# An encoder block on one core: the z of branch A by seven products, three pairs in phases, product sums kept in PSUM

## The chip, the core and the metric

One NeuronCore of a Trainium2 chip runs the whole program. The metric is the time of one execution in microseconds of the device; several runs are made and the median is told. Five engines work beside each other: TensorE (PE in the profile) multiplies matrices into PSUM, VectorE (DVE) and GpSimd (POOL) do elementwise work, ScalarE (ACT) activations and copies, SyncE (SP) issues loads. PSUM has banks of 128 partitions by 512 float32; a product tile here is one of them.

## The reference, cut

One block over 1024 tokens and 16 learned meta tokens, width 1024, float32:

```python
h = concat(meta, x)                      # 1040 x 1024
proj = rmsnorm(h, pre_norm_g) @ w_in + b_in
qa, ka, va, za, qb, kb, vb, zb, ga, gb = split(proj)
oa = diff_attention(qa, ka, va, ...)     # branch A: 4 heads, dense, its result normalised
ob = windowed_gqa(qb, kb, vb, ...)       # branch B: 8 heads, keys within 128
ya = (oa * silu(za)) @ w_out_a
yb = (ob * silu(zb)) @ w_out_b
mixed = sigmoid(ga) * ya + sigmoid(gb) * yb
out = (h + rmsnorm(mixed @ w_out, post_norm_g))[16:]
```

`za` and `zb` have 512 columns, `ga` and `gb` 1024. Meta tokens are needed as keys and values only, not in z, the gates or the output.

## The kernel before

Each float32 matrix product is made of three passes with operands split into a high and a low part (`hi`, `lo`): hi by hi, hi by lo, lo by hi, summed in PSUM. A split is a copy on ACT (`hi`) and a subtraction on another engine (`lo`); the helper `split` (L790) takes that engine as an argument, POOL if none is named. `hn` is the normalised input, transposed, in two parts; `hn[p][1]` holds the second half of the tokens.

The stages in order: norms and projections; branch B, whose gate z is projected as filler; branch A, head by head, with the next head's projections or z of branch B as filler between the steps of the softmax; then, from L720 on, what this change is about:

- **z of branch A** (L900 to L910): four slabs of 128 columns by `proj` (L143), each two chunks of 512 tokens, each chunk 24 matmuls of 128x512 at L151: 192 in all. The first slab takes the PSUM room `mm` of the attention stage, so the scheduler of the framework may put it between the attention's last steps. `gate_a` (L876) makes silu and multiplies with `oa`, which is loaded from `oa_d`.
- **Input sums**, `combos` (L793): the gates are made by a recursion with seven products in place of eight, which wants four sums of blocks of the input, `f1` to `f4` in tiles t1 (f1), t2 (f2), t4 (f4) and t3 (f3). Each is made in two halves of 128x1024 by two or three DVE operations, and split, its lo half on POOL. One piece is taken at each chunk of z.
- **The gates GA and GB** (L913): four pairs of 128-column slabs each, by `seven` (L829). A pair loads four quarters of its weights (two tiles `wr4` of 512 KB), makes sums of them on DVE (`ws`, L837), splits each of seven operands (`wh` on ACT, `wl` on POOL) and runs seven products P1 to P7 of twelve matmuls (L862) into seven PSUM tiles. The products are added up by DVE into SBUF tiles (L871) in the order that the lists SEVEN, FIRST and LAST give, seven sums and one ACT copy (L869) a pair. Before the first P6 the rest of `combos` is run.
- **Mix** (L966) multiplies the gated branches with `w_out_a` and `w_out_b`, and the **output stage** (`out_pair`, L1027) runs four pairs of seven products, then the sum of squares (ACT, L1049), the product with the norm's weights (L1051) and the final product and residual (L1070). The very last product P4 is made in two halves of 256 columns, each in a PSUM tile of its own, and is added on DVE to a tile in SBUF before L1049 reads it.

Engines take their instructions in the program's order; the framework's scheduler sets that order from the order of the code and priorities, and a tile that is written again waits for its readers. In branch B's first block the 16 meta keys are a block of their own: `VBM` and the transposed scores give two products (hi and lo) at L445.

## Time and profile before

| | |
|---|---|
| median of 3 runs | 908.79 us (908.16 to 908.87) |
| profiled execution, time | 907.95 us |
| its span | 906.1 us |
| PE busy | 858.2 us, 95% |
| DVE, ACT, POOL busy | 680.0, 488.8, 380.4 us |
| matmuls | 4670 |

The span is what the hardware profiler sees of one execution; the execution's own time holds a little more around it. PE's clock of 0.990 is its granted mean as a share of full speed (2.4 GHz).

### The profile page before, as it was taken

To read this page: it belongs to the slowest core of one execution; us is meant where nothing else is said; L and a number is where in the kernel's file an instruction comes from. 1 tells how busy PE (TensorE), PEld (TensorE's weight loads), DVE (VectorE), ACT (ScalarE), POOL (GpSimd) and SP (SyncE) were. 2 spreads that over 40 slices of the span, in tenths; PEclk is the share of its full clock that TensorE was granted. 3 is DMA by queue.
4 is the path that set the end of the run, shared out by engine and by line. 5 is a ranking of instruction groups with operands and counts; after the bars stand their busy time and mean duration, and the time that the engine had idled before them with its cause. 6 is when DMAs were issued, how large, how long until landed. Compare 5 with 4: busy or idle time off the path is not lost.

```text
span 906.1 us, 13766 instructions
## 1 busy us (share of the span) xinstructions
PE 858.2 (95%) x4670; PEld 733.9 (81%) x4670; DVE 680.0 (75%) x1432; ACT 488.8 (54%) x975; POOL 380.4 (42%) x482
## 2 busy tenths in 40 slices
PE   4799999999999999999999999399999999999995
PEld 2797988888888898899888887288888888887784
DVE  6735668767988988997877699975444476959897
ACT  4635567766868768877766532344444540114432
POOL 6224543545021212221222189555454555826553
PEclk9999999999999999999999999699999999999998
DMA  8321110215122121021111153464511366311223
GB/s 262 105 50 45 56 57 19 89 43 133 36 71 68 47 72 68 25 71 48 47 65 48 47 185 117 163 210 161 178 56 47 131 231 207 94 63 47 94 95 138
DMA packets 64318, 85.85 MB, mean 95 GB/s; under 512 B 5248, under 2 KB 49294, under 8 KB 64248
## 3 DMA queue, kind: packets, MB, share of 16 engines
q1 hardware_dynamic: 56640, 60.28, 21.1%
q10 hardware_dynamic: 7576, 24.67, 7.9%
q8 instruction: 37, 0.61, 0.3%
q14 instruction: 33, 0.27, 0.1%
q0 software_dynamic: 32, 0.02, 0.0%
HBM read 60.63 MB, written 19.00 MB: 88 GB/s over the span
## 4 chain that ended last, share of the span: by engine, by line
PE 63%; DVE 21%; ACT 7%; issue 5%; POOL 1%; DMA 1%; SPq 0%; DVEq 0%; ACTq 0%; POOLq 0%
PE mm L151 21%; PE pp L862 17%; PE pp L966 9%; PE pv L627 3%; DVE sb L588 3%; PE pv L445 2%; PE pT L432 2%; PE pT L615 2%; PE s L585 2%; DVE sb L598 2%; ACT sb L591 2%; PE s L586 2%; ACT sb L597 1%; DVE ws L837 1%; DVE TB L885 1%
## 5 line engine op out<-in xcount | busy, mean ns | idle before, releaser
L151 PE MATMUL mm<-hn,wh 128*128 128x512 f32 (+2 forms) x896 | 203.6, 356 | 2.9 <-ACT vT L347 1.9
L139 POOL TENSOR_SCALAR wh<-wr 128x256 fp32r<-128x256 f32 x124 | 63.5, 528 | 265.9 <-PE mm L151 237.4
L151 PEld LDWEIGHTS mm<-hn,wh 128*128 128x128 f32 x896 | 145.1, 192 | 19.2 <-ACT vT L347 2.1
L140 POOL TENSOR_TENSOR wl<-wr,wh 128x256 fp32r<-128x256 f32 x124 | 107.4, 890 | 19.4 <-PE mm L151 17.4
L151 PE MATMUL mm<-hn,wl 128*128 128x512 f32 (+2 forms) x448 | 101.5, 353 | 0.0
L792 POOL TENSOR_TENSOR wl<-ws,wh 128x512 fp32r<-128x512 f32 x48 | 71.6, 1501 | 66.0 <-ACT wh L791 52.2
L591 ACT ACTIVATE sb<-sb,st 128x1040 f32<-128x1040 f32 x64 | 74.3, 1162 | 35.2 <-DVE st L588 34.4
L862 PE MATMUL pp<-t,wh 128*128 128x512 f32 (+1 forms) x296 | 73.2, 390 | 15.6 <-ACT wh L791 15.6
L862 PE MATMUL pp<-hn,wh 128*128 128x512 f32 x320 | 79.8, 391 | 0.0
L151 PEld LDWEIGHTS mm<-hn,wl 128*128 128x128 f32 x448 | 73.7, 191 | 7.6
L862 PEld LDWEIGHTS pp<-t,wh 128*128 128x128 f32 x296 | 55.5, 191 | 28.2 <-ACT wh L791 16.9
L588 DVE CUSTOM_DVE_ANT_0 sb<-s,U,st 128x346 f32<-128x346 f32 x128 | 73.1, 574 | 5.8
L871 DVE TENSOR_TENSOR c<-c,pp 128x512 f32<-128x512 f32 x70 | 47.4, 682 | 38.5 <-PE pp L862 36.7
L862 PEld LDWEIGHTS pp<-hn,wh 128*128 128x128 f32 x320 | 60.1, 188 | 13.2
L585 PE MATMUL s<-K,Q 128*128 128x346 f32 (+1 forms) x192 | 65.8, 345 | 0.9 <-DVE st L588 0.4
L586 PE MATMUL s<-K,Q 128*128 128x346 f32 (+1 forms) x192 | 61.3, 321 | 0.0
L598 DVE SCALAR_TENSOR_TENSOR sb<-sb,st 128x1040 f32<-128x1040 f32 x32 | 43.9, 1372 | 13.2 <-ACT sb L597 12.9
L413 ACT ACTIVATE sb<-sb,st 128x385 f32<-128x385 f32 (+2 forms) x64 | 37.5, 588 | 22.6 <-DVE st L410 20.3
L417 POOL TENSOR_SCALAR sb<-sb,st 128x384 f32<-128x384 f32 (+2 forms) x64 | 35.5, 568 | 32.5 <-DVE st L415 32.4
L791 ACT ACTIVATE wh<-ws 128x512 fp32r<-128x512 f32 x48 | 29.7, 625 | 35.0 <-PE pp L862 20.1
L410 DVE CUSTOM_DVE_ANT_0 sb<-s,TB,nsink 128x384 f32<-128x384 f32 (+2 forms) x64 | 35.4, 580 | 16.6 <-PE s L408 15.0
L617 DVE TENSOR_TENSOR al<-pT,ah 128x512 fp32r<-128x512 f32 x64 | 43.7, 686 | 3.6 <-ACT ah L616 2.9
(212 smaller groups left out, 1928.7 us busy)
## 6 DMA issues: line engine op xcount, KB each, us to landing
wr<-in_w_in_dram SPq DMA_DIRECT2D x96, 128.0 KB, 2.5
wr<-in_w_in_dram SPq DMA_DIRECT2D x16, 512.0 KB, 3.6
K<-K ACTq DMA_DIRECT2D x16, 260.0 KB, 3.5
xt<-in_x_dram SPq DMA_DIRECT2D x8, 512.0 KB, 7.1
sg_d<-TB ACTq DMA_DIRECT2D x8, 512.0 KB, 2.6
w<-in_w_out_dram SPq DMA_DIRECT2D x4, 1024.0 KB, 5.5
room<-sg_d SPq DMA_DIRECT2D x8, 512.0 KB, 4.8
fx<-in_x_dram SPq DMA_DIRECT2D x8, 512.0 KB, 4.6
```

Of the source, the lines that this page charges most:

```text
L139: pool.tensor_scalar(hi, raw, 1.0, 1.0, ALU.mult, ALU.mult)
L140: pool.tensor_tensor(lo, raw, hi, ALU.subtract)
L151: pe.matmul(ps[:, :n], lhsT=w[k // 4][:, k % 4, :], rhs=hslice(part, k, st, n), start=(i == 0), stop=(i == 3 * KC - 1))
L585: pe.matmul(s, lhsT=q, rhs=KH[:, m, o:o + n], start=True, stop=False)
L586: pe.matmul(s, lhsT=q, rhs=KL[:, m, o:o + n], start=False, stop=True)
L588: dve.tensor_tensor_reduce(out=sb[:, o:o + n], in0=s, in1=back(U, u0 + o, n), scale=-0.125, scalar=lim, op0=ALU.add, op1=ALU.min, accum_ou ...
L591: act.activation(sb, sb, AF.Exp, bias=st[:, m:m + 1], scale=-1.0, accum_out=st[:, 2 + m:3 + m])
L598: dve.scalar_tensor_tensor(sbs[0], sbs[0], st[:, 4:5], sbs[1], ALU.mult, ALU.add)
L792: lo_eng.tensor_tensor(t[1][:, k], x, t[0][:, k], sub)
L862: pe.matmul(x[n][:, cs], lhsT=w[:, k], rhs=b[n][part][:, k, cs], start=(i == 0), stop=(i == 11))
L871: dve.tensor_tensor(x[o][:, cs], *src, add)
L966: pe.matmul(py, lhsT=w[:, k, :], rhs=g[h][:, k], start=(i == 0), stop=(i == 11))
```

## The change

- z of branch A is made in two pairs of seven products in place of four slabs of two chunks: 168 matmuls in place of 192.
- The two pairs of z and the first pair of GA go in phases: `head` (P1, P2, P3, which use blocks of the input as they are) of all three, then `middle` (P6, P5) of all three, then `tail` (P7, P4). The weights are loaded again for each phase by `quarters`.
- Product sums run on in PSUM: a later product is added onto the bank of an earlier one, which ACT copies out first (`copy`) where its own value is needed. A pair has three DVE sums and three ACT copies in place of seven and one.
- `combos` has t1's and t2's lo halves on DVE, f3 ahead of f4, and is no longer tied to the z chunks.
- Output stage: the first pair in the same phases, the others in the new plain order; the last P4's halves lie in one PSUM tile, and the last result is read out of PSUM.
- Meta keys of branch B: hi and lo stand at partitions 0 and 64 of one operand of 80 rows, so one product does both; POOL zeroes the operands early.

The core of the diff, whose new class takes the place of `seven` and the three lists:

```diff
-    VBM = sbp.tile([MT, 2, P], F32R, tag="am", name="vbm", bufs=1)
+    VBM = sbp.tile([80, 2, P], F32R, tag="sh", name="vbm", bufs=1)
...
-        n, last = 0, 2 * len(blocks) - 1
+        n, last = 0, 2 * len(blocks) - (i > 0)
...
+        if i == 0:
+            pe.matmul(pv[:, :256], lhsT=VBM[:, g, :], rhs=am, start=False, stop=True)
...
-            split(t1, x, k)
+            split(t1, x, k, dve)
...
-            split(t2, x, k)
+            split(t2, x, k, dve)
...
-        for f in (f1, f2, f4, f3):
-            yield from halves(f)
+        halves(f1, True)
+        yield
+        halves(f2, False)
+        yield
+        ys = xs[:]
+        halves(f3, True)
 
         for j in range(2):
             split(t3, xs[j], slice(2 * j, 2 * j + 2))
         yield
+        xs[:] = ys
+        halves(f4, False)
+        yield
...
+        def mul(self, n, ps=None, cuts=(slice(0, H),), done=None):
+
+            old = ps is not None
+            if not old:
+                ps = product()
+            hi, lo = self.operand(n)
+            for cs in cuts:
                 i = 0
                 for w, part in ((hi, 0), (hi, 1), (lo, 0)):
                     for k in range(4):
+                        pe.matmul(ps[:, cs], lhsT=w[:, k], rhs=self.b[n][part][:, k, cs], start=(i == 0 and not old),
+                                  stop=(i == 11), skip_group_check=True)
                         i += 1
+                if done:
+                    self.out(done, ps[:, cs], cs)
+            return ps
...
+        def plain(self, cuts=(slice(0, H),)):
+            X = self.mul("P1")
+            p1 = self.copy(X)
+            self.sum(p1, self.mul("P2"), "c11")
             yield
+            self.mul("P6", X)
+            u2 = self.copy(X)
+            yield
+            Z = self.mul("P5")
+            p5 = self.copy(Z)
+            self.mul("P7", X)
+            self.sum(p5, X, "c22")
+            yield
+            self.mul("P3", Z)
+            self.sum(u2, Z, "c12")
+            yield
+            self.mul("P4", X, cuts, "c21")
+            yield
+
+
+        def head(self):
+            self.X = self.mul("P1")
+            p1 = self.copy(self.X)
+            self.sum(p1, self.mul("P2"), "c11")
+            self.p3 = self.copy(self.mul("P3"))
+
+        def middle(self):
+            self.mul("P6", self.X)
+            uw = self.sum(self.p3, self.X)
+            Z = self.mul("P5")
+            self.p5 = self.copy(Z)
+            self.sum(uw, Z, "c12")
+
+        def tail(self):
+            self.mul("P7", self.X)
+            self.sum(self.p5, self.X, "c22")
+            self.mul("P4", self.X, done="c21")
...
-        run(proj(ZA + P * j, QCH, evac, **({"room": product} if j else {})))
...
+    for n, (col, x) in enumerate(early):
+        x.use(quarters(col))
+        x.head()
+        if n < 2:
+            next(pieces)
+    next(pieces)
+    for col, x in early:
+        x.use(quarters(col))
+        x.middle()
+    next(pieces)
+    for col, x in early:
+        x.use(quarters(col))
+        x.tail()
...
-                (pool if last else dve).tensor_tensor(yb[:, c], v, pg[:, c], ALU.mult)
+                (pool if last and t else dve).tensor_tensor(yb[:, c], v, pg[:, c], ALU.mult)
...
-                if last and n[i] in (1, 3):
+                if last and n[i] > 1:
                     rest.pop(0)()
...
-            return seven(SEVEN if p else FIRST, a, OUT, fp, wsp, result, tmp, cut="P4" if p == 3 else None)
+            pair = Pair(OUT, fp, wsp, result, a, tmp, bufs=4)
+            if p:
+                run(pair.plain((slice(0, H // 2), slice(H // 2, H)) if p == 3 else (slice(0, H),)))
+            else:
+                pair.head()
+                pair.middle()
+                pair.tail()
```

How the change moves instructions, at three places. The first is PE at the end of the attention: `pv` is the last query block's result (L627, L629) and the mean of its squares (L644, L645), `mm` a chunk of z's first slab, `pp` a product tile. Before:

```order
L627 MATMUL pv_6227<-al_6177,V_4387 128x256 x4
L629 MATMUL pv_6227<-am_2577,vm1_128 128x256
L151 MATMUL mm_6317<-hn00_86,wl_6308 128x512 x3
L151 MATMUL mm_6357<-hn01_87,wh_6297 128x512 x3
L644 MATMUL pv_6227<-sh_6256,onesr_126 128x256
L151 MATMUL mm_6357<-hn01_87,wh_6297 128x512
L645 MATMUL pv_6227<-sl_6257,onesr_126 128x256
L151 MATMUL mm_6357<-hn01_87,wh_6307 128x512 x4
L151 MATMUL mm_6357<-hn11_89,wh_6297 128x512 x4
```

The same place on PE in the changed kernel:

```order
L638 MATMUL pv_6226<-al_6176,V_4386 128x256 x4
L640 MATMUL pv_6226<-am_127,vm1_129 128x256
L655 MATMUL pv_6226<-sh_6255,onesr_126 128x256
L656 MATMUL pv_6226<-sl_6256,onesr_126 128x256
L865 MATMUL pp_6303<-hn00_86,wh_6304 128x512 x4
L865 MATMUL pp_6303<-hn10_88,wh_6304 128x512 x4
L865 MATMUL pp_6303<-hn00_86,wl_6305 128x512 x4
```

No z stands between the attention's last products any more; the first product of a pair follows them.

The second is ACT from the attention's last store to the first results (`t10`, `t20` are hi parts of f1 and f2, `wh` hi parts of weights, `c` results of z). Before:

```order
L677 DMA oa_d_84<-oT_5301 128x1024
L791 ACTIVATE t10_6290<-TB_6277 128x1024 x2
L765 ACT_TABLE_LOAD
L766 ACTIVATE c_6352<-mm_6317,binT_78 128x512
L766 ACTIVATE c_6382<-mm_6357,binT_78 128x512
L766 ACTIVATE c_6441<-pp_6408,binT_78 128x512
L791 ACTIVATE t20_6292<-TB_6277 128x1024
```

The same place on ACT in the changed kernel:

```order
L688 DMA oa_d_84<-oT_5300 128x1024
L774 ACTIVATE t10_6289<-TB_6276 128x1024 x2
L774 ACTIVATE wh_6304<-wr4_6299 128x512
L774 ACTIVATE wh_6323<-wr4_6301 128x512
L748 ACT_TABLE_LOAD
L774 ACTIVATE t20_6291<-TB_6276 128x1024
L877 ACTIVATE c_6320<-pp_6303 128x512
L774 ACTIVATE wh_6353<-ws_6351 128x512
```

The weight copies that z's products read are on ACT now, behind the two copies of f1; `proj` had made them on POOL.

The third is PE at the program's last product (`t40`, `t41` are hi and lo of its moving operand). Before, with a tile for each half:

```order
L862 MATMUL pp_9315<-t40_8616,wh_9311 128x256 x4
L862 MATMUL pp_9315<-t41_8617,wh_9311 128x256 x4
L862 MATMUL pp_9315<-t40_8616,wl_9312 128x256 x4
L862 MATMUL pp_9335<-t40_8616,wh_9311 128x256 x4
L862 MATMUL pp_9335<-t41_8617,wh_9311 128x256 x4
L862 MATMUL pp_9335<-t40_8616,wl_9312 128x256 x4
```

In the changed kernel (cut to the rows that differ in kind):

```order
L865 MATMUL pp_9190<-t20_6291,wh_9235 128x512 x4
L865 MATMUL pp_9190<-t21_6292,wh_9235 128x512 x4
L865 MATMUL pp_9190<-t20_6291,wl_9236 128x512 x4
L865 MATMUL pp_9126<-t40_8593,wh_9263 128x256 x4
L865 MATMUL pp_9126<-t41_8594,wh_9263 128x256 x4
L865 MATMUL pp_9126<-t40_8593,wl_9264 128x256 x4
```

P3 now stands ahead of P4; P4's three rows come a second time behind these for the other half, into the same tile.

## Rows read from the trace of the kernel before

**Rows 1.** The page: span, busy time by engine, and two rows of the 40 slices.
```profile
span 906.1 us, 13766 instructions
PE 858.2 (95%) x4670; PEld 733.9 (81%) x4670; DVE 680.0 (75%) x1432; ACT 488.8 (54%) x975; POOL 380.4 (42%) x482
...
PE   4799999999999999999999999399999999999995
...
PEclk9999999999999999999999999699999999999998
```

**Rows 2.** Windows: length, busy us (instructions) of PE, PEld, DVE, ACT, POOL, granted clock, DMA share, GB/s.
```profile
526.60:566.20 39.60, 39.12 (x169) 31.28 (x167) 39.60 (x25) 12.38 (x15) 38.61 (x22) 1.00 0.50 166
566.20:580.90 14.70, 0.01 (x2) 0.01 (x1) 14.70 (x14) 5.33 (x7) 4.99 (x2) 0.64 0.41 138
590.00:640.00 50.00, 50.00 (x221) 41.04 (x220) 33.15 (x38) 23.29 (x36) 26.39 (x20) 1.00 0.54 186
```

**Rows 3.** Timeline of PE: start, us, engine, line, operation, tiles, count, [idle before <- releaser].
```profile
510.09 2.57 PE L151 MATMUL mm<-hn,wh 128*128 128x512 f32 x10
...
580.89 3.45 PE L862 MATMUL pp<-t,wh 128*128 128x512 f32 x8 [14.69 <-ACT wh L791]
...
587.84 1.98 PE L862 MATMUL pp<-hn,wh 128*128 128x512 f32 x8
...
590.56 1.98 PE L862 MATMUL pp<-hn,wh 128*128 128x512 f32 x8
...
596.00 2.03 PE L862 MATMUL pp<-hn,wh 128*128 128x512 f32 x8
...
893.11 1.11 PE L862 MATMUL pp<-t,wh 128*128 128x256 f32 x8
...
895.50 0.64 PE L862 MATMUL pp<-t,wl 128*128 128x256 f32 x4
```

**Rows 4.** Timeline of DVE.
```profile
524.59 0.50 DVE L653 SCALAR_TENSOR_TENSOR oT<-oT,gsub,sq 128x256 f32<-128x256 f32 x1
525.01 2.75 DVE L805 TENSOR_TENSOR TB<-hn,hn 128x1024 f32<-128x1024 f32 x2
...
534.06 3.10 DVE L811 TENSOR_TENSOR TB<-hn,TB 128x1024 f32<-128x1024 f32 x2
537.08 3.42 DVE L812 TENSOR_TENSOR TB<-TB,hn 128x1024 f32<-128x1024 f32 x1
...
566.29 2.35 DVE L821 TENSOR_TENSOR TB<-hn 128x1024 f32<-128x1024 f32 x2
...
580.70 0.68 DVE L837 TENSOR_TENSOR ws<-wr,ws 128x512 f32<-128x512 f32 x1
...
897.61 1.79 DVE L1070 SCALAR_TENSOR_TENSOR fy<-fy,fs,fx 128x512 f32<-128x512 f32 x1
899.32 0.41 DVE L871 TENSOR_TENSOR fy<-c,pp 128x256 f32<-128x256 f32 x1
```

**Rows 5.** Timelines of POOL (the first three) and of ACT.
```profile
536.05 3.36 POOL L792 TENSOR_TENSOR t<-TB,t 128x1024 fp32r<-128x1024 f32 x1
...
580.91 7.84 POOL L792 TENSOR_TENSOR wl<-ws,wh 128x512 fp32r<-128x512 f32 x4 [2.55 <-ACT wh L791]
...
841.20 1.31 POOL L792 TENSOR_TENSOR wl<-ws,wh 128x512 fp32r<-128x512 f32 x1 [3.18 <-ACT wh L791]
...
532.84 1.06 ACT L791 ACTIVATE t<-TB 128x1024 fp32r<-128x1024 f32 x1 [9.66 <-DVE TB L807]
...
580.21 0.63 ACT L791 ACTIVATE wh<-ws 128x512 fp32r<-128x512 f32 x1 [4.06 <-DVE ws L837]
...
899.87 0.42 ACT L1049 ACTIVATE junk<-fy 128x256 f32<-128x256 f32 x1 [1.53 <-DVE fy L871]
```

**Rows 6.** DMA issues between 500 and 600 us: count, KB each, median us to landing.
```profile
wr<-in_w_in_dram SPq DMA_DIRECT2D x5, 512.0 KB, 6.2
```

**Rows 7.** Timeline of PE in branch B's first block: one product of the meta keys.
```profile
194.63 0.38 PE L445 MATMUL pv<-al,vbm 16*128 16x256 f32 x1
```

More of the change, by code (lines that the diff above doesn't have):

```diff
@@ L679, in a_step @@
             late.append(values)
-    am = sbp.tile([80, 256], F32R, tag="am", name="am", bufs=1)
-    zeros(am)
     U = a_table(0)
@@ new lines, in mul, with new, copy, sum @@
+            return ps
+        def new(self, name=None):
+            return (name and self.tmp and self.tmp(name)) or self.room.tile([P, H], F32, tag="c", name="c", bufs=self.bufs)
+        def copy(self, ps):
+            x = self.new()
+            act.activation(x, ps, AF.Copy)
+            return x
+        def sum(self, x, ps, name=None):
+            y = self.new(name)
+            dve.tensor_tensor(y, x, ps, add)
+            if name:
+                self.out(name, y, slice(0, H))
+            return y
@@ new lines, in last @@
+        def last(self):
+            V = self.mul("P4")
+            X = self.mul("P6")
+            p6 = self.copy(X)
+            Z = self.mul("P5")
+            p5 = self.copy(Z)
+            self.mul("P7", X)
+            x = self.copy(X)
+            Y = self.mul("P1")
+            u = self.sum(x, Y)
+            self.sum(u, V, "c21")
+            self.sum(u, p5, "c22")
+            w = self.sum(p6, Y)
+            self.mul("P3", Z)
+            self.sum(w, Z, "c12")
+            self.mul("P2", Y, done="c11")
```

189 lines of the change are left out of this document (89 added, 100 removed).

## The prediction

> **What bounds the kernel now.** I began with the page's totals. TensorE (PE) is busy 858.2 of 906.1 us, VectorE (DVE) 680.0, and in the 40 slices PE shows nines everywhere but in one slice in the middle and at the two ends; its granted clock dips in the same slice [rows 1]. So time can be won in three ways: fewer matmuls, the hole filled, the ends shortened. The windows by stage then say what the hole is [rows 2]. From 526.6 to 566.2 PE is full, and DVE is full too; from 566.2 to 580.9 PE stands still for 14.7 us while DVE works all the time; behind it PE is full again. The hole is DVE's: PE waits until the input sums are made and the weights behind them, and the first product after it runs its eight matmuls in 3.45 us instead of 1.98, at half the clock [rows 3]. Where the hole begins and ends is therefore set by when DVE gets through its sums, and the part of the change that matters is what it gives PE to do until then.
>
> The profiled execution took 907.95 us with a span of 906.1; the median is 908.79. My sum is made against 907.95 and then raised by 0.84.
>
> **The end of the attention.** Before, the first quarter of z (48 matmuls 128x512, the `mm` tiles) lies between the attention's last products, from 510.09 on [rows 3], and PE then goes on without a gap at 526.6. The change replaces z's four slabs by two pairs, so this filler is gone: 48 x 0.227 us (2.72 us per product of twelve, the distance of the starts at 587.84 and 590.56 [rows 3]) = 10.9 us of work leaves cover. What is gained there is little: of the 48 only four stand between the last query block's final products in PE's order, so the last norm ends 4 x 0.227 = 0.9 us earlier than at 525.1, and the first sum (f1) starts at 524.2 [rows 4].
>
> Now ACT's queue. In the changed order the two copies of f1 (`t10`) stand ahead of the first product's weight copy (`wh`), which PE waits for. f1 is six DVE operations of 1.17 us each where nothing disturbs them (2.35 for two [rows 4]), so 524.2 + 7.0 = 531.2; then one `t10` of 1.06 us and a weight copy of 0.63 [rows 5]: PE starts at **532.9**. In the old order f1 took from 525.0 to 534.1 [rows 4], beside POOL; I take the undisturbed price as POOL has nothing to do there in the new order, and the old one as the other end (+2.1). The weights' loads themselves stand behind the load of the fourth `oa_d`, which waits for its store; five such 512 KB loads took 6.2 us to land [rows 6], which puts them at about the same moment, so I add nothing.
>
> **Until the middle.** PE has nine products without input sums (three heads): 9 x 2.72 = 24.5 us, plus 1.5 us for the half clock after ten idle microseconds. Alone that ends at 558.9. What the next product (P6 of the first pair) needs comes from DVE: in the new order there stand, behind f1 and up to P6's operand, 15 operations of 1024 columns (f2, f3, the first of f4, the lo halves of t1 and t2 that POOL did before) and 17 of 512 (eleven weight sums, six of the results). With 1.17 and 0.68 us [rows 4] that is 17.6 + 11.6 = 29.2 us if nothing disturbs them. But POOL disturbs them: an L812 that took 3.42 us lies exactly beside a POOL operation of 3.36 [rows 4, 5]. In the window 526.6 to 566.2, with POOL busy nearly throughout, DVE's 25 operations (13 of the long, 12 of the short kind, 23.4 us alone) took 39.6 [rows 2]: beside POOL it gets on at 0.59. In the new order POOL has nine weight remainders there at 1.96 (7.84 for four, contended) and one lo half of f3 at 3.36 [rows 5], 21.0 us in all. In these DVE does 12.4 us of its work, the other 16.8 alone: 37.8 us. P6's operand is there at 531.2 + 37.8 = 569.0, its copy at **569.7**. So PE waits 569.7 - 558.9 = 10.8 us in all, some of it earlier: the first P3's operand takes 6 x 1.17 + 3 x 0.68 + 1.6 for POOL, so 541.9, its copy 542.5, and PE is there at 539.9; 2.7 us, and 0.8 by the same count for the second P3.
>
> **To the end of the first GA pair.** Twelve products are left, 32.6 us; 1.5 us for the clock after the wait; and the hand-offs in PSUM. P4 must not run onto its bank before DVE has read P7's sum, with only four matmuls (0.9 us) of another product between, three times: a sum of 0.68 [rows 4] and its start cost me 0.5 each, and I add 1.0 for the weights, which each phase loads again (two loads of 512 KB per two products, 5.4 us, is 193 GB/s; 186 GB/s were moved in a stretch without a PE wait [rows 2]). 569.7 + 32.6 + 1.5 + 2.5 = **606.3**. Before, that pair ended at 596.0 [rows 3]. The stage is **10.3 us longer**, although it has 24 matmuls (5.4 us) fewer: those are less than the 10.9 us that lost their cover, and the waiting has not gone, it moved. Ends: no wait at all but for the hand-offs, 532.9 + 57.1 + 1.5 + 2.5 = 594.0, so -2.0 (-4.5 without them); DVE and POOL strictly one after the other is a rival below.
>
> **The steady pairs, 606 to 818.** From 590 to 640 PE is full with DVE at 33.2 of 50 us [rows 2], and the slices show nines as far as the end [rows 1]. Each pair drops four DVE sums (2.7 us) and gains two ACT copies (1.3 at 0.63); both lie beside 7 x 2.72 = 19.0 us of PE, so 0. P6 and P7 now wait for a copy of the bank they run onto, with one whole product (2.72) between: 0, at most +3.
>
> **The end.** Two things. In the last product the half's sum started at 899.32, though its matmuls end by 896.2: it stood behind an L1070 of 1.79 on DVE, and the square then came at 899.87 [rows 3, 4, 5]. Now the square reads PSUM itself. That could give 3.4 us. But both halves now lie in one tile, so the second half's matmuls wait for DVE's read of the first: about 0.3 + 0.41 + 0.5 = 1.2, and the later half leaves its DVE product and the final L1070 where they were. I take **-1.7**, ends -3.0 and +0.5. The Trainium skill (PSUM — Partial Sum Buffer, "PSUM bank collisions raise a hardware error") reports that two engines must not touch one bank and partition quarter at once, different columns or two readers alike, so that DVE and ACT too read that tile one behind the other; no row here shows it, and without any such wait the end would come out at about -3.
>
> **Meta tokens.** One product instead of two per group of the first block: four matmuls of 256 columns fewer. In a row they take half of a 512-column one's 0.227, so 0.11 each; a single one stands there with 0.38 where its end shows [rows 7]. **-0.4**, ends 0 and -1.5. POOL zeroes two more tiles early, beside a full PE: 0.
>
> Sum: 907.95 + 10.3 - 1.7 - 0.4 = 916.15; with 0.84, **917.0**.
>
> **Rivals.**
> *DVE is not disturbed* (faster). If POOL's ten operations cost DVE nothing, because they fall beside sums that read PSUM or into DVE's own pauses, P6's copy is there at 531.2 + 29.2 + 0.6 = 561.0 and PE waits 2.1 us in all: the stage ends at 594.0 + 2.1 = 596.1, and the whole is 907.95 + 0.1 - 2.1 + 0.84 = 906.8; with the hand-offs at nothing 904.3. I put the case at 905.5. It decides when less than a quarter of the 8.6 us that POOL costs is left. For it: POOL has 21.0 us of work there, where it was busy for 38.6 before [rows 2]. Against: the window's 39.6 for 23.4 [rows 2], and the 3.42 [rows 4]. 0.14.
> *A quarter to a half of it* (same). With 2.1 of the 8.6 us left, P6's copy comes at 563.1 and the whole takes 908.9. 0.13.
> *One after the other* (slower still). With 1.31 us for a remainder alone [rows 5], POOL's work is 14.4 us; if DVE stands all that time, P6's operand is at 531.2 + 29.2 + 14.4 = 574.8, 5.8 later: 922.8. 0.11. The Trainium skill (SBUF — State Buffer, "Who interferes with whom") states just this for a DVE operation with two SBUF inputs beside a GpSimd operation that reads SBUF: the loser stands still for the whole of it. The row of 3.42 beside 3.36 agrees; the window's 0.59 I used is what both did together.
> *Hand-offs stall in every pair.* If a bank's copy or sum is 0.3 us late (3.0 for a long DVE operation ahead of it, against 2.72 of cover), four times in seven pairs: +8.4, 925.4. Nothing in the old trace shows it, as no product ran onto a bank then. 0.06.
>
> **How the numbers follow.** My forecast has 0.56: 917.0, by its own terms from 913.6 (end, meta and weights at their good ends) to 921.7 (f1, end and meta at their bad ones). This kernel's measurement can tell about 0.2% (1.8 us) from no change. Slower: 0.56 + 0.11 + 0.06 = 0.73; same 0.13; faster 0.14. The range runs from 904.5, which takes in nearly all of the faster case, to 922, which leaves out the hand-offs and about half of the strict lock.
>
> **What would show it.** Right: PE idle from about 522.5 to 533, released by ACT's weight copy; the clock low behind it; waits before the first P3 products; a wait of about 7 us before the first product on `t2`, ended by ACT `wh` behind a DVE weight sum; the first GA pair done near 606; from the last P4's start to the end about 11.3 instead of 13.0. Wrong: PE full from 533 on, or DVE with idle time before 569; or a PE that already starts near 526.

## The result, and the profile after

| | before | changed |
|---|---|---|
| median | 908.83 us (908.16 to 910.60, 4 runs) | **944.01 us** (942.11 to 946.73, 4 runs) |
| ratio | | 1.0386 (95%: 1.0357 to 1.0416) |
| span of the profiled execution | 906.1 us | 940.3 us |
| matmuls, PE busy | 4670, 858.2 us | 4642, 864.5 us |

Slower, as forecast, but by 35 us and not by 8. The page of the changed kernel, against [rows 1]:

```profile
span 940.3 us, 13654 instructions
...
PE 864.5 (92%) x4642; PEld 736.1 (78%) x4642; DVE 662.1 (70%) x1415; ACT 513.3 (55%) x1020; POOL 367.4 (39%) x458
...
PE   4899999999999999999998296799999999997996
...
PEclk9999999999999999999999688899999999998999
```

The slices show the loss at two places: four slices in the middle below nine in place of one, and a new dip near the end. PE has 28 matmuls fewer and is busy 6 us longer: behind its long waits eight matmuls take 3.6 to 3.8 us and not 1.98, half the clock, and the granted clock of the two early stretches below is 0.78 and 0.83, where it is 1.00 from 640 on. The windows of the changed kernel, with the columns of [rows 2], take the middle apart:

```profile
530.90:574.10 43.20, 29.47 (x108) 22.95 (x108) 36.62 (x33) 15.91 (x22) 30.61 (x11) 0.78 0.37 112
...
600.00:620.00 20.00, 14.92 (x53) 11.71 (x54) 12.65 (x17) 7.43 (x11) 6.05 (x5) 0.83 0.71 250
640.00:700.00 60.00, 60.00 (x264) 49.18 (x263) 20.84 (x26) 28.67 (x46) 29.64 (x22) 1.00 0.38 132
```

(Shown are the stretch up to the middle, one in the tail and one of the steady pairs.) From 600 to 620 no engine is full: the engines wait for each other. From 640 to 700 PE is full. PE's timeline holds the waits (columns of [rows 3]):

```profile
533.09 3.78 PE L865 MATMUL pp<-hn,wh 128*128 128x512 f32 x8 [11.87 <-ACT wh L774]
542.94 2.07 PE L865 MATMUL pp<-hn,wl 128*128 128x512 f32 x4 [6.08 <-POOL wl L775]
...
574.89 3.78 PE L865 MATMUL pp<-t,wh 128*128 128x512 f32 x8 [6.25 <-ACT wh L774]
...
594.95 1.98 PE L865 MATMUL pp<-hn,wh 128*128 128x512 f32 x8
...
604.02 3.78 PE L865 MATMUL pp<-t,wh 128*128 128x512 f32 x8 [5.28 <-DVE c L882]
...
613.41 2.11 PE L865 MATMUL pp<-t,wh 128*128 128x512 f32 x8 [1.06 <-DVE c L882]
...
622.23 0.62 PE L865 MATMUL pp<-hn,wh 128*128 128x512 f32 x2
...
865.71 3.60 PE L865 MATMUL pp<-o,wh 128*128 128x512 f32 x8 [6.31 <-DVE c L882]
...
929.02 1.12 PE L865 MATMUL pp<-t,wh 128*128 128x256 f32 x8
...
931.91 1.22 PE L865 MATMUL pp<-t,wh 128*128 128x256 f32 x8 [1.30 <-DVE fs L162]
```

Marks on PE split the 34.2 us of span. The first GA pair is done at 622.23, of which 1.4 us (six matmuls) belong to the next pair, so at 620.8 against 596.0 [rows 3]: **+24.8**. From there to the start of the last P4 (929.02 against 893.11 [rows 3]) the path is 308.2 us against 297.1: **+11.1**, of which 7.6 lie in the output stage (845.65 to 929.02, against 817.37 to 893.11 before). From the last P4 to the end it is 11.28 against 12.99: **-1.7**.

**The first wait (6.08).** The changed kernel's timeline of DVE, and then that of GpSimd (POOL):

```profile
534.21 1.22 DVE L796 TENSOR_TENSOR TB<-hn,TB 128x1024 f32<-128x1024 f32 x1
535.34 0.68 DVE L838 TENSOR_TENSOR ws<-wr,wr 128x512 f32<-128x512 f32 x1
...
540.56 1.22 DVE L797 TENSOR_TENSOR TB<-TB,hn 128x1024 f32<-128x1024 f32 x1
546.60 1.56 DVE L838 TENSOR_TENSOR ws<-wr,wr 128x512 f32<-128x512 f32 x1 [4.83 <-DMA wr<-in_w_in_dram]
549.40 0.69 DVE L882 TENSOR_TENSOR c<-c,pp 128x512 f32<-128x512 f32 x1 [1.24 <-PE pp L865]
```

```profile
533.11 11.04 POOL L775 TENSOR_TENSOR wl<-wr,wh 128x512 fp32r<-128x512 f32 x2 [66.66 <-ACT wh L774]
```

The first weight remainder was released at 533.11. DVE ran its sums of two SBUF inputs at their undisturbed 1.22 and 0.68 until 541.8, and only when DVE stood still did POOL get through: two remainders took 11.04 us, where one takes 1.31 by itself [rows 5]. DVE stood because the load it waited for had to wait for a weight buffer that the late remainder still had to read (SyncE's queue stood for up to 5.1 us behind a remainder there). So DVE held POOL, POOL held PE and the buffer, and these held DVE.

**The tail's wait (5.28)** is the same kind of loop through queues. The timelines of DVE and of ACT:

```profile
599.61 1.43 DVE L838 TENSOR_TENSOR ws<-wr 128x512 f32<-128x512 f32 x1 [1.50 <-DMA wr<-in_w_in_dram]
600.97 0.68 DVE L998 TENSOR_TENSOR TB<-c,TB 128x512 f32<-128x512 f32 x1
602.68 1.28 DVE L882 TENSOR_TENSOR c<-c,pp 128x512 f32<-128x512 f32 x2 [1.03 <-ACT c L877]
```

```profile
601.68 0.33 ACTq L989 DMA_DIRECT2D ga_d<-TB  x1
602.05 0.60 ACT L877 ACTIVATE c<-pp 128x512 f32<-128x512 f32 x1 [4.22 <-DVE TB L998]
```

DVE waits for a load of weights, ACT's store of the finished z waits for DVE's product (L998), and the copy of a P5 bank waits behind that store. By the order of the code the two sums at 602.68 are the last one of the middle, from the bank that ACT is copying, and behind it the sum of the first pair's P7. The first of them waits for the copy, the second stands behind the first, and P4 may not run onto its bank before the second.

**The output stage (6.31).** DVE's timeline before and after, at the same place of the program:

```profile
819.96 6.85 DVE L792 TENSOR_TENSOR o<-w,o 128x1024 fp32r<-128x1024 f32 x4
826.73 3.46 DVE L792 TENSOR_TENSOR t<-w,t 128x1024 fp32r<-128x1024 f32 x2
```

```profile
848.23 6.84 DVE L775 TENSOR_TENSOR o<-w,o 128x1024 fp32r<-128x1024 f32 x4
854.99 3.46 DVE L775 TENSOR_TENSOR t<-w,t 128x1024 fp32r<-128x1024 f32 x2
...
864.89 0.68 DVE L882 TENSOR_TENSOR c<-c,pp 128x512 f32<-128x512 f32 x1
```

DVE has the same 10.3 us of lo halves in both kernels. Before, PE went on meanwhile into fresh tiles. Now the first pair's P7 stands until the sum at 864.89 has read P6's bank.

### The profile page after: what moved, and what is told of

Read it like the earlier page. It is cut to its first block, busy times and chain, and to the rows that moved or that the text cites. A ratio compares the mean times of both kernels' runs of the same rounds, so it can differ in the third digit from the quotient of the medians.

```text
span 940.3 us, 13654 instructions
## 1 busy us (share of the span) xinstructions
PE 864.5 (92%) x4642; PEld 736.1 (78%) x4642; DVE 662.1 (70%) x1415; ACT 513.3 (55%) x1020; POOL 367.4 (39%) x458
## 4 chain that ended last, share of the span: by engine, by line
PE 60%; DVE 18%; ACT 7%; issue 6%; DMA 6%; POOL 2%; SPq 0%; ACTq 0%; DVEq 0%; POOLq 0%
PE mm L151 20%; PE pp L865 16%; PE pp L1063 7%; DVE ws L838 3%; PE pv L638 3%; DVE sb L599 3%; PE s L596 2%; PE pT L626 2%; PE s L597 2%; PE pT L436 2%; PE pv L454 2%; DMA wr<-in_w_out_b_dram 2%; DMA wr<-in_w_in_dram 2%; DVE sb L609 2%; ACT sb L602 1%
## 5 line engine op out<-in xcount | busy, mean ns | idle before, releaser
L139 POOL TENSOR_SCALAR wh<-wr 128x256 fp32r<-128x256 f32 x108 | 51.7, 494 | 223.5 <-PE mm L151 195.9
L775 POOL TENSOR_TENSOR wl<-ws,wh 128x512 fp32r<-128x512 f32 x56 | 84.9, 1521 | 80.3 <-ACT wh L774 61.6
L865 PE MATMUL pp<-hn,wh 128*128 128x512 f32 x384 | 100.1, 402 | 13.1 <-ACT wh L774 11.9
L865 PE MATMUL pp<-t,wh 128*128 128x512 f32 (+1 forms) x344 | 87.8, 398 | 15.0 <-ACT wh L774 7.1
L865 PEld LDWEIGHTS pp<-hn,wh 128*128 128x128 f32 x384 | 74.3, 194 | 30.5 <-ACT wh L774 12.1
L140 POOL TENSOR_TENSOR wl<-wr,wh 128x256 fp32r<-128x256 f32 x108 | 90.4, 859 | 16.1 <-PE mm L151 14.0
L865 PEld LDWEIGHTS pp<-t,wh 128*128 128x128 f32 x344 | 65.2, 194 | 31.2 <-ACT wh L774 7.9
L775 POOL TENSOR_TENSOR wl<-wr,wh 128x512 fp32r<-128x512 f32 x30 | 49.1, 1644 | 101.2 <-ACT wh L774 79.2
L865 PE MATMUL pp<-hn,wl 128*128 128x512 f32 x192 | 52.7, 397 | 6.1 <-POOL wl L775 6.1
L882 DVE TENSOR_TENSOR c<-c,pp 128x512 f32<-128x512 f32 x35 | 23.7, 682 | 43.3 <-PE pp L865 41.6
## 6 DMA issues: line engine op xcount, KB each, us to landing
w<-in_w_out_dram SPq DMA_DIRECT2D x4, 1024.0 KB, 11.7
```

Source lines behind the costliest of these rows:

```text
L139: pool.tensor_scalar(hi, raw, 1.0, 1.0, ALU.mult, ALU.mult)
L140: pool.tensor_tensor(lo, raw, hi, ALU.subtract)
L775: lo_eng.tensor_tensor(t[1][:, k], x, t[0][:, k], sub)
L865: pe.matmul(ps[:, cs], lhsT=w[:, k], rhs=self.b[n][part][:, k, cs], start=(i == 0 and not old), stop=(i == 11), skip_group_check=True)
```

## The experiments

My theory after the result was that early on DVE and POOL hold each other up, and that behind it and in the output stage the reuse of a bank lets a late DVE or ACT stop PE. Ratios are to the kernel before, run beside each kernel; chips differ (908.8 to 910.2 us for the same kernel), so what one kernel saves against another is worked out from the two ratios, times 909 us. From both intervals (root of the sum of squares) such a difference is uncertain by 3.0 to 3.6 us where the changed kernel is one of the two, and by about 2 us elsewhere. The profiled execution of the changed kernel is the shortest of its four (942.11 us, the median is 944.01), so the same difference read from two traces can come out some 2 us smaller.

### Which part costs what

**z by `proj` again.** The changed kernel with z of A in four slabs, the old `combos` and the first GA pair in the plain order; PSUM sums, output stage and meta product stay.

```diff
-    for n, (col, x) in enumerate(early):
-        x.use(quarters(col))
-        x.head()
...
+    for j in range(4):
...
+        run(proj(ZA + P * j, QCH, evac, **({"room": product} if j else {})))
```

> The z of branch A is made as before (four slabs, the first one as filler at the attention's end), with the input sums taken and split as before, and the first GA pair without phases; the PSUM sums, the output stage and the meta product stay as in the change. Theory 1 (24.8 us of the loss lie between the attention's end and the end of the first GA pair): that pair ends near 596, the whole takes about 919. Rival (the PSUM sums stall the first GA pair as well, as VectorE is behind there): the pair ends 3 to 8 us later, and the whole takes 922 to 927.

917.61 us (1.0094, 1.0079 to 1.0109): against 1.0386 the early stage costs **26.5 us**, and the time is a little below the 919 of theory 1. In PE's timeline the hole is back, and the output stage's wait stays:

```profile
579.50 3.78 PE L856 MATMUL pp<-t,wh 128*128 128x512 f32 x8 [14.69 <-ACT wh L774]
...
840.67 3.75 PE L856 MATMUL pp<-o,wh 128*128 128x512 f32 x8 [6.31 <-DVE c L873]
```

**The whole output stage as before**, on top of that (lists FIRST and SEVEN, separate tiles, old end).

```diff
-            pair = Pair(OUT, fp, wsp, result, a, tmp, bufs=4)
...
+            return seven(SEVEN if p else FIRST, a, OUT, fp, wsp, result, tmp, cut="P4" if p == 3 else None)
```

> The kernel with z as before (917.6), and now the whole output stage as before too: a PSUM tile for each product, VectorE's sums, the last product in two tiles. What is left of the change: PSUM sums in seven gate pairs and the meta product. Theory C (sums in PSUM couple TensorE to a VectorE that is some 10 us behind at the stage's start; undoing the first pair alone only moved the wait of 6.3 us to the second): the wait is gone, 7.6 us less, the end 1.7 more, about 911.7. Rival (the wait comes from ACT's or VectorE's order whatever the tiles): 916 to 919.

909.88 us (1.0007, 0.9995 to 1.0019): **7.9 us** less, and the longest wait of PE in that stage is 0.63. Since the 1.7 gained at the end went as well, the PSUM sums of that stage, with the order of products that goes with them, cost about 9.6. The steady pairs' PSUM sums and the meta product are still in, and nothing is left that can be told from the kernel before.

**Only the first output pair with its own tiles**, in the changed kernel, and on top of z by `proj`:

```diff
+        def first(self):
+            p1 = self.copy(self.mul("P1"))
+            self.sum(p1, self.mul("P2"), "c11")
+            p3 = self.mul("P3")
+            u2 = self.sum(p1, self.mul("P6"))
...
-                pair.head()
-                pair.middle()
-                pair.tail()
+                pair.first()
```

> Only the output stage's first pair is changed back: its seven products each have a PSUM tile of their own and are summed by VectorE, in the order P1 P2 P3 P6 P5 P7 P4. Theory 1 (the 6.3 us wait before P7 there is a hand-off: P7 runs onto the bank of P6, which VectorE reads only after the splits and sums that stand ahead of it): the wait goes and with it the half clock behind it, from the stage's start to the last P4 75.8 us instead of 83.4, the whole about 936.4. Rival (VectorE's splits of that stretch hold the products up whatever the tiles): about 944.

944.96 us (1.0399, 1.0381 to 1.0416).

> Both of the last two undone together: what stays of the change is the PSUM sums in the other pairs, the end in one tile, and the meta product. Theory 1 (the steady pairs cost 2.3 us by waits of their own, the mix 1.2, the end gives 1.7, meta 0.4): about 911. Rival (the waits of 1.2 and 0.9 near 754 and 775 were after-effects of the early stage): about 907, that is 2 us faster than before.

916.28 us (1.0081, 1.0060 to 1.0101). By the ratios that is 1.2 us more and 1.2 us less, neither of which can be told from nothing; z_out lies outside both of its theories. In neither did the 6 us come back. PE's timeline of out_first shows why; the wait went one pair on, to a copy by ACT that comes late out of the same backlog (z_out has the same 5.04 at 851.65):

```profile
877.79 3.78 PE L865 MATMUL pp<-t,wh 128*128 128x512 f32 x8 [5.04 <-ACT c L877]
```

**The filler alone**, on the kernel before: the first z slab may no longer run during the attention.

```diff
-        run(proj(ZA + P * j, QCH, evac, **({"room": product} if j else {})))
+        run(proj(ZA + P * j, QCH, evac, room=product))
```

> The kernel before, with one thing changed: the first slab of branch A's z takes the PSUM room of the product tiles like the other three, so that it can't run between the attention's last steps any more; the number of matmuls stays. Theory G1, the prediction's: the 48 matmuls (10.9 us) lose their cover, of which 0.9 us come back through the earlier last norm; the hole before the first GA product (14.7 us) does not shrink, because VectorE's sums start only when z's chunks let them: 918 to 919 us. Theory G2: the hole is set by when VectorE is through its sums, which begin at the last norm and not at PE's z; the 10.9 us of PE work move behind the attention and fill most of the 14.7 us hole, so that the time changes by 0 to 2 us: 909 to 911 us, and the wait before the first GA product falls from 14.7 to some 4 to 6 us with PE idle of about 10 us at the end of the attention instead. The changed kernel's early stage then lost its 26 us to other things than the filler.

908.27 us (0.9988, 0.9977 to 0.9999): not slower at all, so the 10.9 us of cover were worth nothing. The 14.7 us hole was slack, and the late z filled most of it; at the attention's end PE has no wait above 1.20. PE's timeline of this run has waits of 3.95, 1.69 and 0.75 where the hole was:

```profile
563.33 3.69 PE L151 MATMUL pp<-hn,wh 128*128 128x512 f32 x10 [3.95 <-POOL wh L139]
...
589.31 1.19 PE L862 MATMUL pp<-hn,wl 128*128 128x512 f32 x4 [1.69 <-POOL wl L792]
...
593.98 2.11 PE L862 MATMUL pp<-t,wh 128*128 128x512 f32 x8 [0.75 <-ACT wh L791]
```

### The early stage: which wait, or which work

**The first remainders on DVE.**

```diff
-            split((hi, lo), val[n])
+            split((hi, lo), val[n], lo_eng=self.lo)
...
+    early[0][1].lo = dve
```

> The first two weight remainders of the first z pair are made on VectorE instead of GpSimd. Theory 1 (in the changed kernel GpSimd's first remainder stands still from 533.1 to about 542 because VectorE runs operations with two SBUF inputs without a pause, and the late remainder then also keeps a weight buffer, so that VectorE itself waits 4.8 us for a load): the 6.1 us wait inside the first product goes, VectorE's 4.8 us wait for the load goes, two operations of 0.68 are added to VectorE; the first product of the middle starts near 571.5 instead of 574.9, and the whole takes about 940.5. Rival (VectorE is the only bound of that stretch and the GpSimd wait lies beside it): the middle starts 1.4 us later, not earlier, near 576, and the whole takes 944 to 946.

943.05 us (1.0372, 1.0352 to 1.0391). The 6.08 is gone and the middle starts at 567.78 instead of 574.89, but 1.3 us is all that stays of it, less than these runs can tell. PE's timeline of this run:

```profile
562.25 3.78 PE L865 MATMUL pp<-hn,wh 128*128 128x512 f32 x8 [4.37 <-ACT wh L774]
...
572.41 1.19 PE L865 MATMUL pp<-t,wl 128*128 128x512 f32 x4 [2.53 <-POOL wl L775]
...
600.06 3.78 PE L865 MATMUL pp<-t,wh 128*128 128x512 f32 x8 [4.75 <-DVE c L882]
...
612.16 3.78 PE L865 MATMUL pp<-t,wh 128*128 128x512 f32 x8 [3.51 <-DVE c L882]
```

**P7 and P4 of the early pairs in their own tiles**, added up by DVE.

```diff
-            self.mul("P7", self.X)
-            self.sum(self.p5, self.X, "c22")
-            self.mul("P4", self.X, done="c21")
+            u3 = self.sum(self.u2, self.mul("P7"))
...
+            self.sum(u3, self.mul("P4"), "c21")
```

> The changed kernel with the last phase of the three early pairs summed as before: P7 and P4 go into PSUM tiles of their own, VectorE adds them (two sums and one copy more a pair). Theory A (the 5.3 and 1.1 us waits before P4 are hand-offs: the product may not start before VectorE has read the bank, and VectorE is behind): these waits and the half clock after them go, about 8 us, the whole near 936. Theory B (VectorE, slowed by GpSimd, simply has more to do in this stage than TensorE, so a wait taken away comes back at the next place): 940 to 943.

941.01 us (1.0345, 1.0326 to 1.0363), 3.7 less, as theory B has it. PE's timeline of this run, with the end of the early pairs' last P4 and the next wait:

```profile
611.25 1.07 PE L865 MATMUL pp<-t,wl 128*128 128x512 f32 x4
...
625.70 3.78 PE L865 MATMUL pp<-t,wh 128*128 128x512 f32 x8 [7.80 <-ACT c L877]
```

The waits before P4 are gone, and the early pairs are done at 612.2 in place of 620.8. But PE then stands in the next GA pair for 7.80, for a copy by ACT, and by 632 both kernels have got through the same matmuls. DVE and ACT are late here too; how much of that is the work that this run adds (two sums and a copy a pair, 4.1 us of DVE in all) can't be told.

**A fourth weight buffer.**

```diff
-                r = gp.tile([P, 4, 2 * P], F32, tag="wr4", name="wr4", bufs=3)
+                r = gp.tile([P, 4, 2 * P], F32, tag="wr4", name="wr4", bufs=4)
```

> The changed kernel with four weight buffers of 512 KB in place of three. Theory L1 (the loads hold the early stage back: a load can't start before a late remainder or weight sum has read the old buffer, and VectorE then stands before that load, 4.83 us at 541.8 and 1.50 at 598.1): the waits on those loads go, the tail's wait of 5.28 goes too, 934 to 939 us. Theory L2 (the loads are late only because VectorE and GpSimd are; with the loads earlier the same work still stands before PE): 0 to 2 us less, 942 to 944. Against both: earlier loads beside others may cost something, up to +2.

940.65 us (1.0337, 1.0313 to 1.0361): 4.5 less by the ratios, between the two theories, but 1.0 by the spans of the traces (939.3 against 940.3). In DVE's timeline the first stand has only changed its name. DVE no longer waits for a load; it waits for PE, which waits (6.18) for the same starved remainder:

```profile
549.78 0.69 DVE L882 TENSOR_TENSOR c<-c,pp 128x512 f32<-128x512 f32 x1 [7.65 <-PE pp L865]
```

In the tail DVE has no wait for a load any more, and yet the wait before P4, which L1 forecast gone, is still there. PE's timeline:

```profile
603.95 3.78 PE L865 MATMUL pp<-t,wh 128*128 128x512 f32 x8 [4.18 <-DVE c L882]
```

**Three remedies together** (first remainders on DVE, fourth buffer, own tiles in the first output pair).

> The changed kernel with three remedies together: the first z pair's remainders of P1 and P2 on VectorE, four weight buffers, and the output stage's first pair with separate PSUM tiles. If each alone only moves a wait because another one stands right behind it, together they should give more than the sum of the single ones (lo_dve -1.0, out_first +0.9, wr4_deep its own): 928 to 938 us. If the early stage is bounded by the sum of VectorE's and GpSimd's work, they give no more than the sum of the single ones: 940 to 944, and the rest stays until work is taken away, as no_rem did (-15.6).

939.42 us (1.0313, 1.0287 to 1.0339), 6.6 less, uncertain by 3.6; the single ones sum to 4.6. That they give more together than alone can't be told, and before P4 PE now waits for 8.19 at 604.16.

**Work taken away.** All remainders of the early pairs but one are left out.

```diff
+            if self.still and self.kept:
+                act.activation(hi, val[n], AF.Copy)
+                return hi, self.kept[0]
```

> Leaves out the weight remainders (GpSimd's subtractions) of the three early pairs: one remainder is made, on VectorE, and all their products use it as the low part; the rest of the kernel is the changed one. Theory B1 (VectorE is late because its operations with two SBUF inputs and GpSimd's shut each other out): with GpSimd's 21 remainders gone VectorE works at its own pace of 1.2 and 0.68 us, the first product of the middle starts at 561 to 564 in place of 574.9, and the whole takes 924 to 930. Theory B2 (VectorE's own count of operations, or the weight loads, set the pace): only the 6 us wait inside the first product goes, the middle starts at 570 to 573, and the whole takes 936 to 941.

928.37 us (1.0203, 1.0181 to 1.0226): **16.6 us** less, as theory B1 has it (11.7 by the spans of the traces). PE's timeline of this run, from the first product of the middle, and then one row of DVE's:

```profile
560.71 2.00 PE L872 MATMUL pp<-t,wh 128*128 128x512 f32 x8
...
599.66 3.43 PE L872 MATMUL pp<-t,wh 128*128 128x512 f32 x8 [4.38 <-DVE c L889]
```

```profile
595.79 0.69 DVE L838 TENSOR_TENSOR ws<-wr,wr 128x512 f32<-128x512 f32 x1 [8.18 <-DMA wr<-in_w_in_dram]
```

The middle starts at 560.71 without a wait, 14.2 us earlier. Behind it nothing came back: the first GA pair is done at 610.4, of which 2.0 us (nine matmuls) belong to the next pair, so at 608.4, 47.7 us after the middle's start (45.9 in the changed kernel), although POOL is busy for only 25.3 us from 533 to 620, and not 58.3. The second P4 waits 4.38 for DVE's sum, which stands in DVE's queue behind a wait of 8.18 for a load (by the form of the row, of the next GA pair's weights). The edit takes away three things at once: the contention, PE's waits for remainders, and the buffers that late remainders hold.

**t1's and t2's lo halves on POOL again.**

```diff
-            split(t1, x, k, dve)
+            split(t1, x, k)
```

> The changed kernel with one part undone: the lo halves of t1 and t2 (four subtractions of 128x1024) are on GpSimd again, as in the kernel before. Theory J1 (VectorE is the engine on which the early stage waits): 4 x 1.22 = 4.9 us leave VectorE, the first product and the middle start earlier, 939 to 941 us. Theory J2 (the two engines share one resource, so what matters is the sum of both, and GpSimd's operation of 1024 columns takes longer, 3.36 us, and holds VectorE meanwhile): the first middle product comes later by up to 4 x (3.36 - 1.22) = 8.6 us, half of it under other work, 944 to 952 us. No change (942 to 946) would say that the move did not matter either way.

948.15 us (1.0434, 1.0419 to 1.0450): 4.4 slower. That part of the change was right: the same subtraction took 2.8 us on POOL (5.64 for two) and 1.22 on DVE.

### What kept POOL out

Three small programs that compute nothing of the block: a POOL subtraction released under a run of DVE sums.

```diff
+    for i in range(12):
+        dve.tensor_tensor(o[i], a, c, add)
+        if i == 1:
+            pool.tensor_tensor(wl[1], o[1][:, :H], wh, sub)
```

> Not the block at all but a small program for one question: a GpSimd subtraction of 128x512 (a weight remainder's form) alone; then released after the second of twelve VectorE additions 128x1024 with both inputs in SBUF; then after the second of twelve VectorE additions 128x512 with one input in PSUM; then four GpSimd subtractions in a row with one VectorE addition with two SBUF inputs released by the first. Theory E1 (the two shut each other out as a whole, and an engine that has its next operation ready keeps the other out): the second GpSimd operation lasts until the last of the additions, some 11 us or more, the third 1.3, and the VectorE addition at the end waits for one to three whole GpSimd operations. Theory E2 (they share and slow each other): the second takes 2 to 4 us, and the additions beside it become longer.

The first subtraction, meant to run alone, took 1.57 us, with a DVE sum of 0.68 over its start. Under 12 sums with two SBUF inputs it took 2.17 (one sum took 2.28 in place of 1.22), under sums with one input in PSUM 1.27, with no sum delayed. Beside four subtractions in a row the sum took 1.73 in place of 0.68.

Then four streams, with long and short sums in turn, the release by ACT, and sums that hang on each other:

```diff
+    x = stream("mixed", b[:, :H], (T, H) * 6, False, False)
+    x = stream("byact", x, (T, T) * 6, True, False)
...
+    x = stream("chain", x, (T, H) * 6, True, True)
```

> The small program again, with four streams of twelve VectorE additions with both inputs in SBUF, each with one GpSimd subtraction of 128x512 after the second: (1) long and short ones in turn (128x1024, 128x512), the GpSimd operation released by VectorE; (2) all long, released by a copy on ACT, so at another moment of a VectorE operation; (3) in turn, released by ACT; (4) as (3), each addition reading the result of the one before the last. In the first small program GpSimd got in after one VectorE operation; in the changed kernel it stood for nine. Theory F1 (what differs there is one of these: the sizes in turn, the release by another engine, or the chain): the GpSimd operation lasts 4 us or more in that stream and in those after it, 1.3 to 2.5 in the ones before. Theory F2 (something else of the kernel keeps GpSimd out): 1.3 to 2.5 in all four.

2.10, 1.51, 1.45 and 1.45 us: POOL got in after one sum at most.

Last, the tiles' real shapes and types:

```diff
+    x = stream("long", b[:, :H], False, False)
+    x = stream("short", x, True, False)
+    x = stream("round", x, True, True)
```

> A small program that computes nothing of the block: one GpSimd remainder is released while VectorE runs a stream of sums with two SBUF inputs, in the forms that the changed kernel has there. Stream long has only 128x1024 sums from rounded (float32r) strided inputs, stream short mixes in 128x512 weight sums, stream round adds sums with a rounded output. Theory K1 (GpSimd is kept out by a dense run of VectorE sums of one of these kinds): in at least one stream the remainder ends only when the stream does, so 8 us or more after its release. Theory K2 (it gets in after the operation then running, as in the two small programs so far): 2 to 4 us after the release in all three streams, and one VectorE sum of each stream is longer by 1 us or more. With K2 the nine sums in the changed kernel stay without an explanation.

1.98, **11.54** and 1.85 us. In the middle stream POOL stood until DVE paused. The timelines of micro3, of POOL and of DVE:

```profile
26.52 11.54 POOL L127 TENSOR_TENSOR lo<-wr,hi 128x512 fp32r<-128x512 f32 x1 [13.04 <-ACT hi L126]
```

```profile
27.18 9.16 DVE L130 TENSOR_TENSOR x<-x,h 128x1024 f32<-128x1024 f32 x8
36.26 0.68 DVE L133 TENSOR_TENSOR ws<-ws,wr 128x512 f32<-128x512 f32 x1
38.10 0.69 DVE L137 TENSOR_TENSOR zshort<-lo,x 128x512 f32<-128x512 f32 x1 [1.15 <-POOL lo L127]
```

So a run of DVE sums can keep POOL out to its end, and runs of sums of the same form in the streams before and behind it did not. Nor is it the mixing of short sums that the stream was made for: eight long ones ran in a row there, and the short ones stood ahead of them and behind. Which it will be isn't settled.

### A better order

The kernel before with the hole attacked by the order of things, and with a fourth weight buffer: f3, which only P7 needs, is made last, P4 goes ahead of P7, and the next GA pair's first products fill in.

```diff
+        ("P4", ()),
+        ("P7", (("u3", "u2", "P7"), ("c22", "u3", "P5"), ("c21", "u3", "P4"))))
...
-            if st == QCH[0][0]:
+            if st == QCH[0][0] and j < 3:
...
+            for _ in range(6):
+                next(g0)
...
+            run(g0)
```

> The kernel before, with only this changed: the input sum f3, which P7 alone needs, is made after the first GA pair's weight sums instead of ahead of them; that pair runs P1 P2 P6 P5 P3 P4 P7, with P1 and P2 of the next pair ahead of its P7; a fourth weight buffer. Theory D (the hole of 14.7 us is TensorE waiting for sums that its next five products do not need): P6 starts near 572 in place of 580.9, TensorE then has 16 us of products until f3's split is done near 587, and the whole takes about 899, 8 to 10 us less than before. Rival (VectorE's total is the bound, so the wait comes back before P7 and before the second pair's P6): 904 to 907.

906.45 us (0.9968, 0.9949 to 0.9987): 14.69 of hole became waits of 3.31, 1.85 and 2.10, and the time is in the rival's range.

Then f3 behind P4's operand, three products of the next pair ahead of P7, and eight result buffers (the edit against p7):

```diff
-                  steps=SEVEN if p else P7LAST, between={} if p else {"P4": pieces})
+                  steps=P7LAST if p == 0 else SEVEN)
...
+            run(pieces)
...
+            next(g)
```

> The kernel of the run p7, with f3's sums and split later still: after the weight copy of P4, and with three products of the second GA pair (P1 P2 P6) ahead of the first pair's P7; eight result buffers. Theory D (the 2.1 us wait before P4 and the 1.85 us wait for a remainder stood behind f3's split on ACT and GpSimd): both go, about 5 us with the clock, and the whole takes 901 to 904. Rival (VectorE's total is the bound, the wait moves on to the second pair's P6): 905 to 907.

905.65 us (0.9955, 0.9939 to 0.9971), again in the rival's range.

And the one meta product of the change on top:

```diff
+        if i == 0:
+            pe.matmul(pv[:, :256], lhsT=VBM[:, g, :], rhs=am, start=False, stop=True)
```

> The kernel of the run p7b, and with the one product for the meta keys of branch B. Four matmuls of 256 columns fewer: 0.4 us less than p7b if TensorE is what that block waits for, no difference if not; with two more copies and subtractions for the second set of rows up to 1 us more.

**903.63 us** (0.9934, 0.9918 to 0.9949), the fastest: 6.0 us under the kernel before by the ratio. The meta product's share is 1.9, uncertain by 2.0. In the old hole's window ([rows 2]: PE busy 0.01 of 14.70) PE now works for 12.18:

```profile
566.20:580.90 14.70, 12.18 (x39) 9.18 (x40) 14.68 (x14) 5.09 (x8) 8.82 (x5) 0.77 0.20 61
```

## Why the prediction was right or wrong

The sum forecast +8.2 on the profiled execution; the span grew by 34.2. The 26.0 between lie so:

- **The end of the attention: right.** First product at 533.09 (forecast 532.9), its eight matmuls at half the clock (3.78).
- **"So PE waits 10.8 us in all", "its copy at 569.7": 5.2 us short.** DVE's own work was sized well: from 530.9 to 574.1 it was busy 36.62 us (forecast 37.8). It stood for the other 6.6, the idle time before 569 that the prediction named as a sign against it: I took DVE as the engine that loses beside POOL and never as the one that starves POOL, and so had no wait of PE for a remainder (6.08) and no way back from it to DVE. The forecast waits before the first P3 products did not come. The wait of 6.25 before the middle then came as described, behind a weight sum of DVE. no_rem shows that the remainders are the cause: without them the middle starts at 560.71, as the rival "DVE is not disturbed" has it (561.0). Of these 14.2 us the forecast had 8.6; the other 5.6 are about what it was short of.
- **"the hand-offs in PSUM ... 2.5": 9.3 us short, the step that failed.** From the middle's start to the end of the stage I allowed 36.6 us (32.6 + 1.5 + 2.5); it took 45.9. Most of it is one hand-off: the first pair's P4 waits 5.28, and its twelve matmuls then take 5.29 us (604.02 to 609.31) and not 2.72. I priced a hand-off by DVE's sum itself (0.5) and left out what stands ahead of that sum in DVE's queue, and ahead of the copy in ACT's; my sum counts DVE's work up to the middle's first operand and none behind it. The runs point to that backlog, and not to the bank alone. With tiles of their own (sep_tail) the early pairs took 37.2 us, close to the 36.6, and the next pair stood for 7.80 instead. Without remainders (no_rem) the stretch took 47.7. What the backlog is made of isn't settled: DVE's and ACT's own work, or the weights loaded a third time. In no_rem DVE stood for 8.18 before the load that follows these; in wr4_deep it stood for no load in the tail, and P4 still waited 4.18. No run loads them less often.
- **The output stage, not priced at all, so put at nothing without a reason: 7.6 us**, shown by out_old (7.9). The rival "hand-offs stall in every pair" had the mechanism at the wrong place: it wants a backlog on DVE, and the steady pairs have next to none.
- **The steady pairs to the mix, 0 (at most +3): +2.3; mix: +1.2.** A wait of 1.23 for DVE's sum and one of 0.91 for a weight copy on POOL lie there; no run tests either.
- **The end -1.7: right** (11.28 us; the second half waits 1.30 for DVE's read, forecast 1.2). The Trainium skill's rule on two engines in one bank (PSUM — Partial Sum Buffer) stays untested: DVE does read each half behind ACT's square (931.44 behind 930.76, 934.26 behind 933.75), as the rule would have it, but no run takes such a wait away.
- **Meta -0.4:** together with the four matmuls fewer (-0.9) it should bring the start of f1 forward by 1.3; DVE begins it at 523.99, 1.0 earlier than [rows 4]. Nearer to nothing here, but the first product starts anywhere from 532.00 (lo_dve) to 534.34 (fix_all) in kernels that are alike up to there, so one pair of traces can't tell; 1.9 in the p7b pair, where the interval holds both.
- **"those are less than the 10.9 us that lost their cover": wrong as a reason.** no_fill lost the same cover at no cost, because the hole behind it took the work up. The changed kernel's PE does stand for 11.87 before 533.09, but the middle comes when DVE is through, whenever PE begins. The stage is longer by what DVE, ACT, POOL and the banks do in it.

The rival "one after the other" (922.8) had the Trainium skill beside it (SBUF — State Buffer, "Who interferes with whom"). The runs agree that the loser stands still (micro: a DVE sum of 2.28 in place of 1.22 beside a subtraction), and that a sum with an input in PSUM disturbs nothing (1.27). They go beyond the Trainium skill in one point: by its rule the loser waits for the whole of one instruction, and here it waited for a row of them (11.04 for two remainders, 11.54 in micro3).

## What to carry over

Adding a product onto an old PSUM bank saves a sum, but ties PE to the reader's whole queue: do it where the reader has no backlog (the steady pairs: no difference told in out_old), and not behind 10 us of splits (the output stage: 9.6 us). A wait taken away is worth little while the engine behind it is late (sep_tail: 3.7 us): look for work to take away. Before calling lost filler a cost, look for slack behind it that takes the work up. And a hole that is set by input sums is best closed by asking which product needs which sum: making the last-needed one last, with the next pair's products ahead of it and deeper buffers, gave 4.1 us (p7b).

## What the runs showed that I had not expected

A GpSimd subtraction of 1.3 us stood for 8.7 us under nine DVE operations that all ran at their undisturbed times, and one in a small program 10 us, while the other seven under such sums in the small programs got in after one sum at most. And 28 matmuls fewer made PE busier by 6.3 us, because behind the long waits the granted clock was down: eight matmuls took 3.78 us there and 1.98 without a wait.
